# Two-layer trunk: the handovers between mixer and MLP issued in another order

## The chip, the cores and the metric

The kernel runs on one NeuronCore of a Trainium2 chip. Its metric is the time of one execution on the device, in microseconds (us). Three executions before the change took 1163.44, 1163.95 and 1166.36 us; the median is 1163.95.

## The reference, cut to what matters

512 tokens of 1024 features pass two residual layers. Layer 0 mixes the tokens by latent attention with 16 heads, layer 1 by an mLSTM with 4 heads; after each mixer stands an MLP.

```python
for i in range(DEPTH):                       # 0: attention, 1: mLSTM
    x = x + mixer_i(rms_norm(x, norm_mix[i]))        # ends in  ... @ w_o
    x = x + square(relu(rms_norm(x, norm_ffn[i]) @ w1[i])) @ w2[i]   # 1024 -> 4096 -> 1024
```

`rms_norm(x, g)` is `x * rsqrt(mean(x*x) + 1e-6) * g`. The mLSTM's head output is normalised the same way, per head, and multiplied by a sigmoid gate before `w_o`.

## The kernel before, in words

**Numbers and tiles.** Everything is fp32. A product is made of three matmuls in a rounded format: each operand is split into a high part (a copy, on ScalarE) and a low part (what is left, a subtraction on VectorE), and the three products high by high, high by low, low by high are summed (`mm3`). So each weight tile of 128x1024 goes through a load (SyncE queue, tag `wr`, 3 buffers), a copy to `wh` and a subtraction to `wl` (3 buffers each), and each activation through the same two steps.

**The residual stream** lies in `xs[t, f]`: four blocks of 128 tokens by two halves of 512 features. A matmul needs the features on the partitions, so at each handover TensorE turns `xs` by transposes against the identity (`turn`). `Norm.half(th, m)` turns the features of m and m+1 for the two token blocks of half `th` into one PSUM bank (4 transposes), and then, for each of the two features' 256 columns, copies them out on ScalarE with the gain (`hi`) and subtracts on VectorE (`lo`). `Norm.square(t, f)` sums the squares of one `xs` tile on ScalarE; `stat` and a reciprocal or power make the factor of the norm from the sums, which is applied after the product, to its rows.

**Handover from mixer to MLP** (`out_proj`, then the head of `ffn`). `out_proj` multiplies by `w_o` in two halves f of the output; `z0`, `z1` are the four PSUM banks of each half (`mm` has 3 banks, `tp` 4, `po` 1). In layer 0 most of half 0 (`zo`) was done beside the attention. A last loop over the four token blocks t finishes both halves, adds them to `xs`, takes the squares, starts the first `w1` tile after t = 0 and turns the first two blocks after t = 2. `norm.tail` holds the turns of the last two blocks; `ffn` does these around the first products: `w1` tiles 0 and 1 by token halves (`HALVES`), then whole tiles in the loop over `units`: F units (one `w1` tile: 24 matmuls of 512 columns) and P units (one of the seven products of a block scheme on `w2`, 24 matmuls of 512 columns). In that loop `ahead` loads and splits weights two to four units early, `f_post` takes relu and square, GpSimd sums the parts that the scheme needs, and `y_add` adds a product to `xs` with the factor `r2`.

**Handover from MLP to mLSTM.** The last `w2` block runs as four plain products (`l_mm`), n = 0 to 3, of two token blocks each; the first turns for the mLSTM (`half(0, ...)`, `half(1, (0, 2))`) stand between them, the rest in `mlstm` after the first value product. In layer 1 the same places turn the result for the output (`out`).

**The mLSTM's heads** end in a normalisation: the numerators' sums go through a chain of small instructions on VectorE and GpSimd, `hb` is scaled, and 8 transposes turn it (line 1146) for the output projection.

**What sets the order.** Instructions issued through `ipe`, `idve`, `iact`, `ipool` (while on) stay behind the instruction that the program issued before them on the same engine. All others are placed by a planner in the framework, by simulated times; it also assigns the buffers. The framework makes two instructions on the same PSUM bank wait for each other when they run on different engines. `ipe` and `idve` are always on, `iact` in the last loop of `out_proj`, in `ffn` and around the tail in `mlstm`. The loads stand on the SyncE queue in the planner's order.

Of the kernel before, what the change touches and what calls it, by code (L numbers as in the profile page):

```python
# [61 lines left out]
def trunk(ctx: ExitStack, tc, a, yT, dbg=None):  # L62
# [173 lines left out]
    class Norm:  # L236
# [13 lines left out]
        def half(self, th, m, bank=ps_mm):  # L250

            ps, c = bank(), HALVES[th]
            for n in range(2):
                for t in range(2):
                    turn(ps, (2 * n + t) * P, m + n, 2 * th + t)
            for n in range(2):
                g, p_ = cst[:, self.gcol + m + n:self.gcol + m + n + 1], ps[:, n * 256:(n + 1) * 256]
                hi, lo = self.hi[m + n], self.lo[m + n]
                iact.activation(hi[:, c], p_, AF.Copy, scale=g)
                idve.scalar_tensor_tensor(lo[:, c], p_, g, hi.bitcast(F32)[:, c], op0=mult, op1=sub)  # L260
# [28 lines left out]
    def mla(mp):  # L289
# [378 lines left out]
        out_proj(a["w_oa"], oT, 0, zo, wo[3])  # L668
# [6 lines left out]
    def out_proj(wsrc, lhs, layer, z0=None, w0=None):  # L675
# [7 lines left out]
        for j in range(3):  # L683
            for f, z in todo:
                w = load_w(wsrc[f, j], D)
                for t in range(NB):
                    for k in (2 * j, 2 * j + 1):
                        o_mm(z[t], w, k, t, lhs, ipe)
        last = [(z0, w0, (KD - 1,)) if w0 else (z0, load_w(wsrc[0, 3], D), (KD - 2, KD - 1)),
                (z1, load_w(wsrc[1, 3], D), (KD - 2, KD - 1))]  # L690
        norm = Norm(C_NF + layer * KD)
        iact.on = True
        for t in range(NB):
            for z, w, ks in last:
                for k in ks:
                    o_mm(z[t], w, k, t, lhs, ipe)
            for f, (z, _, _) in enumerate(last):
                idve.tensor_add(xs[t, f], xs[t, f], z[t])
            if t == 0:
                norm.first = split_w(load_raw(a["w1"][layer, 0], D), D, iact, idve)  # L700
            elif t == 2:
                for m in range(0, KD, 2):
                    norm.half(0, m)
            for f in range(2):
                norm.square(t, f)
        norm.tail = [lambda m=m: norm.half(1, m, ps_tp) for m in range(0, KD, 2)]
        iact.on = False
        norms.append(norm)

# [3 lines left out]
    def ffn(fp, layer, last):  # L713
# [166 lines left out]
        ws["F", 0] = norm.first  # L880
        f_load(1)
# [3 lines left out]
        for do in norm.tail[:2]:  # L885
            do()
        f_split(1)
        f_mm(ps[1], 1, HALVES[0])
        for do in norm.tail[2:]:
            do()  # L890
        u_ = norm.stat()
        idve.reciprocal(r2, u_)
# [12 lines left out]
        for s_ in range(2, len(units)):  # L905
# [11 lines left out]
            if u[0] == "F":  # L917
                f_post(ps, u[1])
            else:
# [26 lines left out]
        for n, (th, f) in enumerate(((0, 0), (0, 1), (1, 0), (1, 1))):  # L946
            bank["L", f] = [ps_tp(), ps_tp()]
            for t in range(2):
# [23 lines left out]
    def mlstm(lp):  # L972
# [62 lines left out]
        for h in range(MH):  # L1035
# [7 lines left out]
            for t in range(NB):  # L1043
# [97 lines left out]
            nc.vector.tensor_scalar_mul(gh, cst[:, C_HN + 2 * h:C_HN + 2 * h + 2], 0.5)  # L1141
            for n in range(2):
# [10 lines left out]
        out_proj(a["w_ob"], [(out_h[m // 4][:, m % 4], out_l[m // 4][:, m % 4]) for m in range(KD)], 1)  # L1153
# [100 lines left out]
```

## Time and profile before

| | before |
|---|---|
| median of three executions | 1163.95 us |
| the profiled execution's own time | 1163.95 us |
| its span, first to last instruction | 1161.9 us |
| TensorE matmuls busy | 1121.3 us, 97% |
| VectorE busy | 826.9 us, 71% |
| ScalarE busy | 556.4 us, 48% |
| GpSimd busy | 455.7 us, 39% |
| mean granted TensorE clock | 0.994 of full speed |

Busy time is the union of an engine's instructions; what is left of the span is the time in which the engine stood. Matmuls overlap, so the distance between the starts of two like groups tells more than the duration of one. The rows on which the prediction rests stand two sections below.

### The profile page before, as it was taken

Reading aid. Unit: us, or ns where it says so; the run is one execution under the profiler, and the core shown is the slowest. Engines: PE = TensorE matmul, PEld = TensorE weight load, DVE = VectorE, ACT = ScalarE, POOL = GpSimd, SP = SyncE. Lnnn points to the kernel's source line nnn. Section 1 sums busy time; section 2 is a strip of 40 time slices with the busy share of each in tenths; the row PEclk is TensorE's granted clock in tenths of the full one; section 3 lists DMA queues with packets and bytes.
Section 4 is the critical chain, followed back from the end, with each engine's and each line's share of the span. In section 5 each row is a group of like instructions: output and inputs, shape, how many; then the busy total and the mean of one; then the engine's idle time right before and its main releaser. Section 6 shows DMA issues by size and latency. Waiting matters only on the chain.

```text
span 1161.9 us, 15626 instructions
## 1 busy us (share of the span) xinstructions
PE 1121.3 (97%) x5802; PEld 954.0 (82%) x5802; DVE 826.9 (71%) x1284; ACT 556.4 (48%) x969; POOL 455.7 (39%) x453
## 2 busy tenths in 40 slices
PE   7899999989999999999999999989899999999998
PEld 7889987878888888888788898877788888888886
DVE  7689997356798789778666565534478788779863
ACT  4578776345544435444454343323454444444451
POOL 6677775107356337434001011100255347436500
PEclk9999999999999999999999999999999999999999
DMA  5301111423432343343113222322532433343212
GB/s 200 111 24 47 37 56 46 137 73 128 127 104 79 108 124 89 96 111 108 37 56 90 73 73 73 91 59 69 162 92 74 127 109 91 91 127 94 70 55 73
DMA packets 32427, 104.27 MB, mean 90 GB/s; under 512 B 3424, under 2 KB 6752, under 8 KB 32352
## 3 DMA queue, kind: packets, MB, share of 16 engines
q1 hardware_dynamic: 32352, 103.27, 29.3%
q8 instruction: 46, 0.75, 0.3%
q14 instruction: 29, 0.24, 0.1%
HBM read 101.16 MB, written 2.10 MB: 89 GB/s over the span
## 4 chain that ended last, share of the span: by engine, by line
PE 89%; DVE 4%; ACT 2%; POOL 2%; issue 1%; DMA 1%; SPq 0%; ACTq 0%; POOLq 0%; DVEq 0%
PE mm L80 38%; PE tp L80 36%; PE mm L174 4%; PE mm L176 4%; PE mm L175 3%; PE po L80 3%; DVE xg L80 1%; DVE wl L80 1%; ACT xg L80 1%; DVE x L80 1%; PE tp L176 1%; PE tp L175 1%; PE tp L174 1%; ACT t L80 1%; POOL x L80 0%
## 5 line engine op out<-in xcount | busy, mean ns | idle before, releaser
L80 PE MATMUL mm<-xg,wh 128*128 128x512 f32 (+1 forms) x1088 | 322.9, 380 | 7.4 <-ACT wh L80 7.1
L80 POOL TENSOR_TENSOR z<-z 128x256 f32<-128x256 f32 x112 | 131.4, 1193 | 344.7 <-ACT z L80 342.5
L80 PEld LDWEIGHTS mm<-xg,wh 128*128 128x128 f32 x1088 | 202.7, 191 | 46.0 <-ACT wh L80 7.6
L80 DVE TENSOR_TENSOR wl<-tw,wh 128x1024 fp32r<-128x1024 f32 x102 | 173.1, 1697 | 74.2 <-ACT wh L80 74.2
L80 PE MATMUL mm<-xg,wl 128*128 128x512 f32 (+1 forms) x544 | 207.9, 382 | 1.5 <-DVE wl L80 1.5
L80 POOL TENSOR_TENSOR tw<-tw,tw 128x1024 f32<-128x1024 f32 x56 | 158.9, 2846 | 30.4 <-issue 29.2
L80 PE MATMUL tp<-wh,hl 128*128 128x512 f32 x424 | 165.2, 390 | 0.5 <-DVE hl L80 0.5
L80 PE MATMUL tp<-wh,hh 128*128 128x512 f32 x424 | 165.4, 390 | 0.0
L80 PE MATMUL tp<-wl,hh 128*128 128x512 f32 x424 | 165.0, 389 | 0.0
L80 DVE TENSOR_TENSOR wl<-wr,wh 128x1024 fp32r<-128x1024 f32 (+1 forms) x72 | 121.3, 1685 | 49.9 <-ACT wh L80 49.9
L80 DVE SCALAR_TENSOR_TENSOR x<-tp,r,x 128x512 f32<-128x512 f32 (+1 forms) x215 | 149.5, 733 | 9.0 <-PE tp L80 8.8
L80 ACT ACTIVATE t<-mm 128x512 f32<-128x512 f32 (+3 forms) x97 | 54.3, 560 | 200.9 <-PE mm L80 191.8
L80 ACT CAST wh<-tw 128x1024 fp32r<-128x1024 f32 x102 | 106.8, 1047 | 36.7 <-PE tp L80 28.9
L80 PEld LDWEIGHTS mm<-xg,wl 128*128 128x128 f32 x544 | 103.7, 191 | 24.8 <-DVE wl L80 6.5
L164 DVE TENSOR_TENSOR wl<-wr,wh 128x1024 fp32r<-128x1024 f32 (+2 forms) x44 | 52.7, 1199 | 60.8 <-ACT wh L160 60.7
L80 PEld LDWEIGHTS tp<-wh,hl 128*128 128x128 f32 x424 | 79.6, 188 | 18.0 <-DVE hl L80 1.4
L80 ACT CAST wh<-wr 128x1024 fp32r<-128x1024 f32 (+1 forms) x74 | 78.8, 1065 | 32.1 <-PE tp L80 27.7
L80 PEld LDWEIGHTS tp<-wh,hh 128*128 128x128 f32 x424 | 79.6, 188 | 17.1 <-issue 0.8
L80 PEld LDWEIGHTS tp<-wl,hh 128*128 128x128 f32 x424 | 79.6, 188 | 16.4
L80 DVE TENSOR_TENSOR hl<-z,hh 128x1024 fp32r<-128x1024 f32 (+1 forms) x60 | 85.2, 1420 | 3.4 <-ACT hh L80 3.4
L160 ACT CAST wh<-wr 128x1024 fp32r<-128x1024 f32 (+2 forms) x44 | 43.9, 997 | 87.3 <-PE po L80 31.3
L80 ACT CAST hh<-z 128x1024 fp32r<-128x1024 f32 (+1 forms) x60 | 56.9, 949 | 57.2 <-POOL z L80 57.2
(271 smaller groups left out, 2041.9 us busy)
## 6 DMA issues: line engine op xcount, KB each, us to landing
wr<-in_w SPq DMA_DIRECT2D x64, 512.0 KB, 3.6
tw<-in_w SPq DMA_DIRECT2D x64, 512.0 KB, 3.6
wr<-in_w_qkv SPq DMA_DIRECT2D x8, 640.0 KB, 4.0
wr<-in_w_oa SPq DMA_DIRECT2D x8, 512.0 KB, 3.7
wr<-in_w_mo SPq DMA_DIRECT2D x8, 512.0 KB, 3.6
wr<-in_w_ob SPq DMA_DIRECT2D x8, 512.0 KB, 3.6
wr<-in_w_v SPq DMA_DIRECT2D x6, 512.0 KB, 4.0
wr<-in_w_z SPq DMA_DIRECT2D x8, 336.0 KB, 4.8
```

What stands on the lines that cost most here:

```text
L80: return lambda *args, **kw: tc.keep_in_program_order(f(*args, **kw)) if self.on else f(*args, **kw)
L160: act.copy(hi[:, :n], raw[:, :n])
L164: dve.tensor_sub(lo[:, :n], raw[:, :n], hi[:, :n].bitcast(F32))
L174: pe.matmul(out, lhsT=lh, rhs=rh, start=start, stop=False)
L175: pe.matmul(out, lhsT=lh, rhs=rl, start=False, stop=False)
L176: pe.matmul(out, lhsT=ll, rhs=rh, start=False, stop=stop)
```

## The change

No computation is added or left out; instructions stand elsewhere.

1. `Norm.half`: both ScalarE copies of a bank come before both VectorE subtractions (before: copy, subtraction, copy, subtraction).
2. `out_proj` becomes a generator that yields after each weight tile; its loops run over f outside and j inside. Without a given `w0` (layer 1) that tile is split into a buffer of another tag (`big`).
3. Last loop of `out_proj`: two `w1` tiles are split there (after t = 0 and t = 1), not one; only block 0 is squared; the turns of m = 6 move from after t = 2 to between the two halves of t = 3.
4. Head of `ffn`: all four tail turns after the first half unit; the split of the second tile is gone from here. The squares of blocks 1 to 3 follow the posts of F units 2 to 4, the reciprocal `r2` the last of them.
5. End of `ffn`: `y_add` comes before the turns; the four turns of half 0 are shared between t = 0 and t = 1 of n = 2; the squares move to n = 3 and, for the last two, into `mlstm` behind the tail. The `w2` tile `b21` is split into the tag `z`, not `wh`/`wl`.
6. `mlstm`, last head: `out_proj` is started before the last transposes, with its first weight tile (24 matmuls); these transposes are kept in program order behind it.

```diff
@@ Norm.half
-            for n in range(2):
-                g, p_ = ...
-                hi, lo = self.hi[m + n], self.lo[m + n]
+            parts = [(self.hi[m + n], self.lo[m + n], cst[...], ps[:, n * 256:(n + 1) * 256]) for n in range(2)]
+            for hi, lo, g, p_ in parts:
                 iact.activation(hi[:, c], p_, AF.Copy, scale=g)
+            for hi, lo, g, p_ in parts:
                 idve.scalar_tensor_tensor(lo[:, c], p_, g, hi.bitcast(F32)[:, c], op0=mult, op1=sub)
@@ out_proj
-        for j in range(3):
-            for f, z in todo:
+        for f, z in todo:
+            for j in range(3):
                 w = load_w(wsrc[f, j], D)
                 for t in range(NB):
                     for k in (2 * j, 2 * j + 1):
                         o_mm(z[t], w, k, t, lhs, ipe)
-        last = [(z0, w0, (KD - 1,)) if w0 else (z0, load_w(wsrc[0, 3], D), (KD - 2, KD - 1)),
-                (z1, load_w(wsrc[1, 3], D), (KD - 2, KD - 1))]
+                yield
+        if not w0:
+            w0 = split_w(load_raw(wsrc[0, 3], D), D, to=big(F32R).rearrange("p (c j) e -> c p (j e)", c=2))
+            ks = (KD - 2, KD - 1)
+        else:
+            ks = (KD - 1,)
+        last = [(z0, w0, ks), (z1, load_w(wsrc[1, 3], D), (KD - 2, KD - 1))]
...
         for t in range(NB):
-            for z, w, ks in last:
+            for f, (z, w, ks) in enumerate(last):
                 for k in ks:
                     o_mm(z[t], w, k, t, lhs, ipe)
+                if t == 3 and f == 0:
+                    norm.half(0, 6)
             for f, (z, _, _) in enumerate(last):
                 idve.tensor_add(xs[t, f], xs[t, f], z[t])
-            if t == 0:
-                norm.first = split_w(load_raw(a["w1"][layer, 0], D), D, iact, idve)
+            if t < 2:
+                norm.first.append(split_w(load_raw(a["w1"][layer, 2 * t], D), D, iact, idve))
+                for f in range(2 - 2 * t):
+                    norm.square(t, f)
             elif t == 2:
-                for m in range(0, KD, 2):
+                for m in (0, 2, 4):
                     norm.half(0, m)
-            for f in range(2):
-                norm.square(t, f)
@@ ffn, head
-        ws["F", 0] = norm.first
-        f_load(1)
+        ws["F", 0], ws["F", 1] = norm.first
         f_load(2)
         ps = [ps_mm(), ps_mm()]
         f_mm(ps[0], 0, HALVES[0])
-        for do in norm.tail[:2]:
+        for do in norm.tail:
             do()
-        f_split(1)
         f_mm(ps[1], 1, HALVES[0])
-        for do in norm.tail[2:]:
-            do()
-        u_ = norm.stat()
-        idve.reciprocal(r2, u_)
@@ ffn, loop over units
                 f_post(ps, u[1])
+                if s_ < 5:
+                    norm.square(s_ - 1, 0)
+                    norm.square(s_ - 1, 1)
+                    if s_ == 4:
+                        idve.reciprocal(r2, norm.stat())
...
-                        l_split("b21", False)
+                        l_split("b21", True)
@@ ffn, end
-                if n == 2 and t == 0:
-                    half(0, (0, 2, 4, 6))
+                y_add(2 * th + t, f, bank["L", f][t])
+                if n == 2:
+                    half(0, ((0, 2), (4, 6))[t])
                 if n == 3 and t == 0:
                     half(1, (0, 2))
-                y_add(2 * th + t, f, bank["L", f][t])
-                if not last:
-                    nxt.square(2 * th + t, f)
+                if not last and n < 2:
+                    nxt.square(t, f)
+                if not last and n == 3:
+                    nxt.square(2 + t, 0)
@@ mlstm, after the first value product
                     for do in norm.tail:
                         do()
+                    for i in range(2):
+                        norm.square(2 + i, 1)
@@ mlstm, end of a head
+            if h == MH - 1:
+                proj_b = out_proj(a["w_ob"], [(out_h..., out_l...) for m in range(KD)], 1)
+                next(proj_b)
             for n in range(2):
...
-                    pe.transpose(ps[:, i * P:(i + 1) * P], hb[i // 2][:, o:o + P], ident)
+                    (ipe if h == MH - 1 else pe).transpose(ps[:, i * P:(i + 1) * P], hb[i // 2][:, o:o + P], ident)
...
-        out_proj(a["w_ob"], [(out_h..., out_l...) for m in range(KD)], 1)
+        for _ in proj_b:
+            pass
```

## Rows read from the trace of the kernel before

**Rows 1.** The page: busy time of each engine, share of span, instructions.

```profile
PE 1121.3 (97%) x5802; PEld 954.0 (82%) x5802; DVE 826.9 (71%) x1284; ACT 556.4 (48%) x969; POOL 455.7 (39%) x453
```

**Rows 2.** Windows: stretch, its us, busy of PE PEld DVE ACT POOL, PEclk, DMA.

```profile
239.94:265.50 25.56, 19.69 (x138) 18.23 (x137) 12.38 (x25) 13.51 (x29) 0.00 (x0) 0.93 0.26 78
254.00:256.00 2.00, 1.90 (x9) 1.90 (x10) 0.05 (x1) 0.00 (x0) 0.00 (x0) 0.50 0.51 80
258.17:258.96 0.79, 0.79 (x11) 0.79 (x9) 0.00 (x0) 0.16 (x1) 0.00 (x0) 1.00 0.00 0
262.64:265.50 2.86, 2.86 (x26) 2.86 (x25) 1.60 (x2) 2.19 (x4) 0.00 (x0) 1.00 0.25 36
285.00:577.89 292.89, 292.89 (x1285) 240.44 (x1284) 233.03 (x210) 137.25 (x167) 128.03 (x75) 1.00 0.33 98
577.89:593.01 15.12, 11.45 (x61) 9.27 (x60) 8.58 (x15) 8.47 (x18) 0.91 (x2) 1.00 0.22 69
593.01:757.22 164.21, 164.20 (x983) 145.59 (x981) 95.17 (x240) 67.06 (x132) 18.36 (x29) 1.00 0.25 75
757.22:769.07 11.85, 8.28 (x33) 6.75 (x34) 4.93 (x16) 2.08 (x5) 1.01 (x1) 0.86 0.11 39
805.15:831.43 26.28, 20.68 (x141) 18.95 (x140) 12.50 (x25) 13.62 (x29) 0.00 (x0) 0.94 0.23 63
```

**Rows 3.** Timeline, TensorE, first MLP handover: start, us, [idle before <- releaser].

```profile
242.74 0.63 PE L80 MATMUL mm<-cst,x 128*128 128x128 f32 x4 [1.33 <-DVE xg L80]
...
252.84 0.51 PE L80 MATMUL mm<-xg,wh 128*128 128x256 f32 x2 [3.64 <-ACT wh L80]
254.10 0.58 PE L80 MATMUL mm<-xg,wl 128*128 128x256 f32 x1 [0.75 <-DVE wl L80]
```

**Rows 4.** Waits of TensorE, second MLP handover, 805 to 832 us.

```profile
PE mm L80 <- ACT wh L80: 3.5, 1, 3.5
```

**Rows 5.** Timeline, all engines, the copies of the turned banks.

```profile
241.60 0.84 ACT L80 ACTIVATE xg<-mm,cst 128x256 fp32r<-128x256 f32 x2 [0.55 <-DVE xg L80]
242.11 0.88 DVE L80 SCALAR_TENSOR_TENSOR xg<-mm,cst,xg 128x256 fp32r<-128x256 f32 x2 [0.54 <-ACT xg L80]
...
243.02 0.47 ACT L80 ACTIVATE xg<-mm,cst 128x256 fp32r<-128x256 f32 x1 [0.58 <-DVE xg L80]
```

**Rows 6.** Timeline, SyncE queue, ahead of the second MLP handover.

```profile
788.16 13.79 SPq L150 DMA_DIRECT2D wr<-in_w  x3
```

**Rows 7.** Timeline, all engines, handover from MLP to mLSTM.

```profile
580.69 0.30 PE L80 MATMUL mm<-cst,x 128*128 128x128 f32 x1 [1.33 <-DVE xg L80]
...
585.43 1.22 DVE L164 TENSOR_TENSOR wl<-wr,wh 128x1024 fp32r<-128x1024 f32 x1
...
587.98 1.40 DVE L80 SCALAR_TENSOR_TENSOR x<-tp,r,x 128x512 f32<-128x512 f32 x2
...
588.87 0.30 PE L80 MATMUL mm<-cst,x 128*128 128x128 f32 x1 [2.08 <-DVE x L80]
```

**Rows 8.** Timeline, all engines, the last head's transposes.

```profile
760.79 1.14 PE L1146 MATMUL tp<-cst,hb 128*128 128x128 f32 x8 [3.59 <-DVE hb L1139]
```

**Rows 9.** Chain that ended last, start of the mLSTM's output projection.

```profile
761.93 5.74 PE mm L80 x18
767.67 1.40 PE po L80 x6
```

**Rows 10.** Groups, ScalarE: the squares, all 24; busy, mean ns.

```profile
L80 ACT ACTIVATE t<-x 128x512 f32<-128x512 f32 x24 | 15.1, 628 | 21.6 <-DVE x L80 21.6
```

**Rows 11.** Timeline, all engines, ahead of the first P unit.

```profile
277.38 3.38 POOL L80 TENSOR_TENSOR tw<-tw,tw 128x1024 f32<-128x1024 f32 x1
...
278.86 2.98 DVE L80 TENSOR_TENSOR wl<-wr,wh 128x1024 fp32r<-128x1024 f32 x1 [0.36 <-ACT wh L80]
...
283.31 0.50 PE L80 MATMUL tp<-wh,hl 128*128 128x512 f32 x1 [0.16 <-DVE hl L80]
```

**Rows 12.** Waits of TensorE, end of the kernel, 1144 to 1162 us.

```profile
PE mm L80 <- DVE x L80: 1.5, 3, 0.9
```

More of the change, by code (lines that the diff above doesn't have):

```diff
@@ L255, in half @@
                     turn(ps, (2 * n + t) * P, m + n, 2 * th + t)
-            for n in range(2):
-                g, p_ = cst[:, self.gcol + m + n:self.gcol + m + n + 1], ps[:, n * 256:(n + 1) * 256]
-                hi, lo = self.hi[m + n], self.lo[m + n]
+            parts = [(self.hi[m + n], self.lo[m + n], cst[:, self.gcol + m + n:self.gcol + m + n + 1],
+                      ps[:, n * 256:(n + 1) * 256]) for n in range(2)]
+            for hi, lo, g, p_ in parts:
                 iact.activation(hi[:, c], p_, AF.Copy, scale=g)
+            for hi, lo, g, p_ in parts:
                 idve.scalar_tensor_tensor(lo[:, c], p_, g, hi.bitcast(F32)[:, c], op0=mult, op1=sub)
@@ L667, in mla @@
         load_x()
-        out_proj(a["w_oa"], oT, 0, zo, wo[3])
+        for _ in out_proj(a["w_oa"], oT, 0, zo, wo[3]):
+            pass
     def o_mm(ps, w, k, t, lhs, pe=nc.tensor):
@@ L688, in out_proj @@
                         o_mm(z[t], w, k, t, lhs, ipe)
-        last = [(z0, w0, (KD - 1,)) if w0 else (z0, load_w(wsrc[0, 3], D), (KD - 2, KD - 1)),
-                (z1, load_w(wsrc[1, 3], D), (KD - 2, KD - 1))]
+                yield
[5 more added lines that the diff above has]
+        last = [(z0, w0, ks), (z1, load_w(wsrc[1, 3], D), (KD - 2, KD - 1))]
         norm = Norm(C_NF + layer * KD)
+        norm.first = []
         iact.on = True
         for t in range(NB):
-            for z, w, ks in last:
+            for f, (z, w, ks) in enumerate(last):
                 for k in ks:
                     o_mm(z[t], w, k, t, lhs, ipe)
+                if t == 3 and f == 0:
+                    norm.half(0, 6)
             for f, (z, _, _) in enumerate(last):
                 idve.tensor_add(xs[t, f], xs[t, f], z[t])
-            if t == 0:
-                norm.first = split_w(load_raw(a["w1"][layer, 0], D), D, iact, idve)
+            if t < 2:
+                norm.first.append(split_w(load_raw(a["w1"][layer, 2 * t], D), D, iact, idve))
+                for f in range(2 - 2 * t):
+                    norm.square(t, f)
             elif t == 2:
-                for m in range(0, KD, 2):
+                for m in (0, 2, 4):
                     norm.half(0, m)
-            for f in range(2):
-                norm.square(t, f)
         norm.tail = [lambda m=m: norm.half(1, m, ps_tp) for m in range(0, KD, 2)]
@@ L708, in out_proj @@
         norms.append(norm)
+        yield
     norms = []
@@ L1141, in mlstm @@
             nc.vector.tensor_scalar_mul(gh, cst[:, C_HN + 2 * h:C_HN + 2 * h + 2], 0.5)
+            if h == MH - 1:
+                proj_b = out_proj(a["w_ob"], [(out_h[m // 4][:, m % 4], out_l[m // 4][:, m % 4]) for m in range(KD)], 1)
+                next(proj_b)
             for n in range(2):
@@ L1152, in mlstm @@
                 nc.vector.scalar_tensor_tensor(ol, t_, gh[:, n:n + 1], oh.bitcast(F32), op0=mult, op1=sub)
-        out_proj(a["w_ob"], [(out_h[m // 4][:, m % 4], out_l[m // 4][:, m % 4]) for m in range(KD)], 1)
+        for _ in proj_b:
+            pass
     with stage("mlap") as pool:
```

## The prediction

> **What bounds the kernel now.** I read four views. The page first: TensorE is busy for 1121.3 of the 1161.9 us of the span, the next engine for 826.9 [rows 1]. So only the 40.6 us in which TensorE stands, and what a lowered clock adds, can be won by moving work. The windows second, one for each stage, to see where it stands: in the first MLP's loop (285.00 to 577.89) and in the mLSTM (593.01 to 757.22) it never does; four short stretches hold it, the two handovers from mixer to MLP (25.56 and 26.28 us long), the one from MLP to mLSTM (15.12) and the end of the last head (11.85) [rows 2]. Third, TensorE's timeline and waits within these: what ended each gap [rows 3, 4, 7, 8]. Last, ScalarE and VectorE in the same moments, for what those had in front of them [rows 5, 7, 11]. The change touches just these four stretches, the squares and the kernel's end.
>
> **Prices.** Eight turns take 0.79 us, so one 0.1; a half unit of 24 matmuls of 256 columns takes 2.86 [rows 2]; six matmuls of 512 columns take 1.40, so one 0.233 [rows 9]. TensorE's clock: in 254 to 256 us, behind the gap of 3.64 us, the granted clock is 0.50, the 1.2 GHz level, where the stretches without a gap have 1.00 [rows 2, 3]; behind the last head's gap 18 matmuls take 5.74 us where three times 1.40 would be 4.20, so such a gap costs some 1.5 us more than itself [rows 9].
>
> **Part 1, copies grouped.** Today ScalarE's copy waits 0.55 us for VectorE's subtraction of the same bank, and that 0.54 us for the copy; from one pair of copies to the next, a bank, pass 1.42 us (241.60 to 243.02) [rows 5]. Grouped, a bank costs ScalarE 0.84 and VectorE 0.88, on different banks at once: 0.9 a bank, four banks in 4.4 us in place of some 6.3. By itself that moves nothing; it decides what the next parts wait for.
>
> **Parts 3 and 4, handover to the first MLP (239.94 to 265.50).** TensorE's work in it: 32 turns (3.2), the products of t = 3 (9 matmuls, 2.1), four half units (11.4): 16.7 us of 25.56. It loses 1.33 at the turns of m = 6, which want a fourth `mm` bank, and 3.64 + 0.75 at the second half unit, whose weight's copy and subtraction stand behind the tail's copies [rows 3]; the rest is the low clock behind that. After the change I lay it out from 239.94: 12 turns to 241.2; the three products of half 0 at t = 3 to 241.9; the bank of m = 0, turned at 240.4, comes free at 242.4 (its copies 0.84, its subtractions 0.88, some 0.3 of handing over), so a wait of 0.5 stays; turns and six products to 244.3; half unit to 247.2; 16 turns to 248.8; the second half unit to 251.6, its weight split by 240.1, since the `wh` buffer comes free when the last loop begins; the tail's eight half copies are done by 252.0, the second-half products take feature after feature from 251.6, so nothing waits; two half units more: the first whole unit starts at 257.4, not 265.5. **Gain 8.1.** Bounds: 4.4 if only the wait for the weight goes, 8.9 if no wait stays.
>
> **The same for the second MLP (805.15 to 831.43).** The wait for the weight is 3.5 [rows 4]. Twelve products at t = 3 (2.8), 3.2 and 11.4 make 17.4; six products stand before the turns of m = 6, so their bank is free in time; 0.3 of small waits: 17.7 of 26.28. **Gain 8.6**, bounds 3.5 and 8.9. Its loads: by 801.6 all of the first four `w1` tiles were issued (the second at 788.16, three issues in 13.79 us) [rows 6], ahead of the handover, so the earlier split finds its data, and the next loads come no later, since they wait for subtractions that come earlier. Nothing on GpSimd's queue moves: its sums begin behind the post of F unit 1, which stays.
>
> **Part 5, handover to the mLSTM (577.89 to 593.01).** Three groups of 12 products (8.4) and 24 turns (2.4) are 10.8 of 15.12 us. Lost: 1.33 for the fourth bank, and 2.08 and more at 588.87, where the turns of half 1 wait for `y_add`, which stood behind two weight subtractions (1.22 each) and three of the turns' own on VectorE [rows 7]. With two banks, 2.8 us of products, then two banks, no bank is awaited; with `y_add` ahead of the copies (0.7 each [rows 7]) the sums that half 1 turns are done some 2.7 us before it. The mLSTM's own weights may still put one subtraction of 1.22 there; that slack covers it. **Gain 4.3**, bounds 1.3 and 4.6. The squares moved behind the tail feed factors for blocks 2 and 3, which are used two value products (some 6 us) later than block 0's; two squares are 1.3 us: no cost. `b21` in another buffer lets the first value weights be split early: no cost, no term.
>
> **Part 6, last head.** TensorE waits 3.59 us for `hb` [rows 8]. 24 matmuls are 5.6 us, longer than the wait. At 761.93 they start without a wait for their weight [rows 9]; that it is there 4.7 us earlier I take, since it is the stage's first; the lower bound is for the case that it isn't. 5.6 + 0.8 stand for the 11.85 us from 757.22 to 769.07 [rows 2], where turns and the same 24 matmuls ran, half of them at the low clock. **Gain 5.4**, bounds 0 (the matmuls don't run there) and 5.4. The other order of f and j costs nothing: one weight per 5.6 us either way.
>
> **End of the kernel.** Three waits for `y_add`, 1.5 in all [rows 12]; the last, before the final turns, stays; two go, and the turns stand better. **Gain 1.0**, bounds 0 (the output copies still wait for buffers) and 1.5.
>
> **What the squares cost.** In each MLP six squares of 0.63 us [rows 10] move to F units 2 to 4, behind the post, ahead of the next copy on ScalarE's in-order queue. Two take 1.3 us with their reads. Behind unit 3 this has no cover: today ScalarE's copy of the next weight comes straight after the post, VectorE's subtraction runs 278.86 to 281.84, the second one follows, and the first P unit already waits 0.16 for it at 283.31 [rows 11]. Moved by 1.3 it waits 1.3 longer. **Cost 1.3 in each MLP, 2.6.** Bounds: 0, if the subtraction meets less of GpSimd's work and shortens from 2.98 toward the 1.22 that the same form takes at 585.43 [rows 7, 11]; 3.1, if it meets as much again (1.3 + 1.76). I take 1.3, the value between, since GpSimd's instruction of 3.38 lies before the subtraction as well as beside it [rows 11].
>
> The Trainium skill's page "SBUF — State Buffer", "Who interferes with whom", says that a VectorE instruction with two SBUF inputs and a GpSimd instruction that reads SBUF exclude each other, the later one waiting for the whole of the earlier. The row of 2.98 beside GpSimd's 3.38 agrees with waiting. By that rule a shift of 1.3 us can fall on either side of one GpSimd instruction, so it speaks for the upper bound as much as for 0; that case is the second rival.
>
> **The sum.** 8.1 + 8.6 + 4.3 + 5.4 + 1.0 - 2.6 = 24.8. The profiled execution's own time is 1163.95, the median of the runs: 1163.95 - 24.8 = 1139.1, forecast **1139**.
>
> **Rivals.**
> 1. *The re-plan uncovers the mLSTM* (slower than before). Its 983 matmuls and most VectorE instructions are placed by the planner, and all start some 11 us earlier in its simulation, with other buffers free. For: the last head shows what a bare chain costs, 3.59 + 1.5 = 5.1 us. Against: the stretch has no idle time now [rows 2], its order follows program priorities, and its first products are the same. Place: the chains between projections, scores, numerators and transposes. Each that is uncovered costs 5.1; from five on the change loses (5 x 5.1 = 25.5). With eight, two in each head: 1180.
> 2. *The first P unit waits longer*: 3.1 in each MLP in place of 1.3 gives 1142.7; if the lateness also reaches the second P unit (GpSimd's sums to ScalarE to VectorE), up to 1145.
> 3. *The low clock stays.* The new handovers put 16 turns in a row, and their waits of 0.2 to 0.5 us are not the only ones. If the clock falls to 1.2 GHz there as behind the old gaps, 1.5 us in each of four places: 1145. Against: it was 1.00 over the 24 turns and the 2.08 us gap of the mLSTM handover [rows 2, 7].
> 4. *The last head's matmuls don't cover it* (their bank or weight is late, so that the change doesn't do what it says there): 5.4 lost, 1144.5. Against: they are held behind the last numerator only, and `mm` and `po` are then free.
>
> **How the numbers follow.** Forecast with its own range 1135 to 1142: 0.57. Rival 2: 0.14; rival 3: 0.09; rival 4: 0.06; of rival 1 one to three chains (1144 to 1154) 0.05, four or five (1160 to 1165) 0.02, more 0.03. The rest, 0.04, has the squares at no cost and the upper bounds of the gains (1133 to 1135). The range of eight in ten, 1133 to 1148, takes in the forecast and rivals 2 to 4, with room for a part that each mis-sizes, and leaves out most of rival 1. About 0.3%, 3.5 us, is what can be told from no change. Faster by more than that 0.95 (all but rival 1's far parts), the same 0.02 (four or five chains), slower 0.03.
>
> **What would show it.** Right: the two MLP handovers are 17 to 18 us from the end of t = 2 to the first whole unit, with no wait for `wh`; the second half unit runs at clock 1.00; a bank's copies come 0.9 apart; behind the last numerator come projection matmuls, and no wait on line 1146; the mLSTM handover is about 10.8. The squares: a wait of some 1.5 us for `hl` at the first P unit of each MLP. Wrong: a wait for `xg` or `x` longer than 1 us in a handover, idle time in the mLSTM, a P unit waiting 3 us, or a stretch of clock 0.5 behind 805 us.

## The result, and the profile after

The changed kernel takes 1137.05 us (median of four executions, 1136.99 to 1137.65), the kernel before beside it 1164.96 (four, 1163.44 to 1166.36): a ratio of 0.9762, interval 0.9745 to 0.9779. The forecast was 1139, its range 1133 to 1148. The profiled execution took 1137.65 us with a span of 1135.8; the spans differ by 26.1 us, the own times by 26.3, where the sum said 24.8. That execution is the slowest of its four, 0.6 us above their median.

The page after, busy time of each engine ([rows 1] before):

```profile
PE 1113.4 (98%) x5802; PEld 949.7 (84%) x5802; DVE 824.1 (73%) x1284; ACT 553.0 (49%) x969; POOL 455.1 (40%) x453
```

The instruction counts are the same. TensorE stands for 22.4 us of the span, where it stood for 40.6.

Windows of the kernel after, in the columns of [rows 2]:

```profile
240.01:257.63 17.62, 17.32 (x138) 16.54 (x137) 10.65 (x23) 9.26 (x20) 0.00 (x0) 1.00 0.41 138
257.63:273.98 16.35, 16.35 (x74) 13.53 (x73) 9.86 (x6) 11.38 (x20) 13.48 (x8) 1.00 0.44 161
273.98:570.43 296.45, 296.02 (x1297) 242.63 (x1296) 237.60 (x216) 141.53 (x175) 131.24 (x78) 1.00 0.33 100
570.43:581.27 10.84, 10.84 (x62) 9.29 (x60) 8.28 (x16) 6.98 (x17) 0.91 (x2) 1.00 0.17 48
581.31:745.50 164.19, 164.19 (x984) 145.78 (x983) 94.00 (x238) 66.69 (x133) 18.45 (x29) 1.00 0.26 75
745.50:751.90 6.40, 6.40 (x33) 5.31 (x32) 2.60 (x12) 1.56 (x4) 1.01 (x1) 1.00 0.15 61
787.96:805.86 17.90, 17.90 (x142) 17.19 (x140) 9.95 (x21) 9.26 (x20) 0.00 (x0) 1.00 0.37 118
```

The first, fourth, sixth and last of these are the four stretches that held TensorE's idle time. They are 17.62, 10.84, 6.40 and 17.90 us, where they were 25.56, 15.12, 11.85 and 26.28. In three of them busy time equals length, and the granted clock is 1.00 in all (it was 0.93, 1.00, 0.86 and 0.94). The mLSTM is as long as before, 164.19 for 164.21.

TensorE's timeline in the first MLP handover of the kernel after. It answers to [rows 3]:

```profile
242.54 0.63 PE L80 MATMUL mm<-cst,x 128*128 128x128 f32 x4 [0.30 <-DVE xg L80]
...
247.26 1.91 PE L80 MATMUL tp<-cst,x 128*128 128x128 f32 x16
```

The 1.33 us for a bank have become 0.30, and the waits for the second weight, 3.64 and 0.75, are gone: behind the 16 turns nothing is awaited. ScalarE and VectorE in the same moments, the rows that answer to [rows 5]:

```profile
240.65 2.29 ACT L80 ACTIVATE xg<-mm,cst 128x256 fp32r<-128x256 f32 x6 [2.19 <-PE mm L80]
...
241.52 2.44 DVE L80 SCALAR_TENSOR_TENSOR xg<-mm,cst,xg 128x256 fp32r<-128x256 f32 x6
```

Three banks go through without a stop: 2.29 / 3 = 0.76 us a bank on ScalarE, 0.81 on VectorE, where a pair of copies came every 1.42 us.

The last head, TensorE ([rows 8] before), and the first and last turns of the output, after and then before:

```profile
745.28 0.39 PE L80 MATMUL mm<-wh,big 128*128 128x512 f32 x1
...
750.87 1.03 PE L80 MATMUL tp<-cst,hb 128*128 128x128 f32 x8
...
1118.99 1.03 PE L80 MATMUL mm<-cst,x 128*128 128x128 f32 x8
...
1131.39 0.63 PE L80 MATMUL mm<-cst,x 128*128 128x128 f32 x4 [0.93 <-DVE x L80]
```

```profile
1144.05 1.93 PE L80 MATMUL mm<-cst,x 128*128 128x128 f32 x16
...
1157.50 0.63 PE L80 MATMUL mm<-cst,x 128*128 128x128 f32 x4 [0.94 <-DVE x L80]
```

The projection's 24 matmuls start straight behind the last numerator, the turns follow them without a wait. At the end only the wait before the last turns is left; 13.45 us from the first turns to the last are now 12.40.

What got worse is small: from the first whole F unit to the mLSTM handover, second and third window, 312.80 us (before 312.39, from [rows 2]: 265.50 to 577.89), and 313.13 in the second MLP, 805.86 to 1118.99 (before 312.62, 831.43 to 1144.05). All engines ahead of the first P unit after, against [rows 11]:

```profile
266.76 2.99 DVE L80 TENSOR_TENSOR wl<-tw,wh 128x1024 fp32r<-128x1024 f32 x1 [3.53 <-ACT wh L80]
...
269.83 3.32 POOL L80 TENSOR_TENSOR tw<-tw,tw 128x1024 f32<-128x1024 f32 x1 [1.16 <-DVE wl L80]
...
272.26 1.97 DVE L80 TENSOR_TENSOR wl<-wr,wh 128x1024 fp32r<-128x1024 f32 x1 [1.38 <-ACT wh L80]
...
275.71 0.50 PE L80 MATMUL tp<-wh,hl 128*128 128x512 f32 x1 [0.43 <-DVE hl L80]
```

The P unit waits 0.43 us where it waited 0.16, and 0.87 in the second MLP (0.36 before). Not all of the 0.87 is the squares'. In this execution GpSimd stood 1.31 us in the second MLP for a load (before: 1.13); in the profile of the changed kernel run again (last line) it did not, and the wait is 0.47:

```profile
815.77 6.05 POOL L80 TENSOR_TENSOR tw<-tw,tw 128x1024 f32<-128x1024 f32 x2 [1.31 <-DMA tw<-in_w]
...
820.49 2.41 DVE L80 TENSOR_TENSOR wl<-wr,wh 128x1024 fp32r<-128x1024 f32 x1 [0.94 <-ACT wh L80]
...
824.37 0.50 PE L80 MATMUL tp<-wh,hl 128*128 128x512 f32 x1 [0.87 <-DVE hl L80]
```

```profile
823.37 0.50 PE L80 MATMUL tp<-wh,hl 128*128 128x512 f32 x1 [0.47 <-DVE hl L80]
```

By the two profiles the squares cost 0.3 us in the first MLP and 0.1 to 0.5 in the second, not 1.3 each; the runs on the squares below narrow the second to about 0.3.

| term of the sum | predicted | measured in the traces |
|---|---|---|
| handover to the first MLP | 8.1 | 25.56 - 17.62 = 7.9 |
| handover to the second MLP | 8.6 | 26.28 - 17.90 = 8.4 |
| handover to the mLSTM | 4.3 | 15.12 - 10.84 = 4.3 |
| last head | 5.4 | 11.85 - 6.40 = 5.4 |
| end of the kernel | 1.0 | 13.45 - 12.40 = 1.0 |
| squares | -2.6 | -0.4 - 0.5 = -0.9 |
| sum | 24.8 | 26.1 |

The row of the squares is what both MLPs have lost in length, and its second number holds the late load too. In the other profile of the changed kernel the same stretches are 312.75 and 312.84 us long, 0.4 and 0.2 more than before.

### The profile page after: what moved, and what is told of

Read it like the earlier page. It is cut to its first block, busy times and chain, and to the rows that moved or that the text cites. A ratio compares the mean times of both kernels' runs of the same rounds, so it can differ in the third digit from the quotient of the medians.

```text
span 1135.8 us, 15650 instructions
## 1 busy us (share of the span) xinstructions
PE 1113.4 (98%) x5802; PEld 949.7 (84%) x5802; DVE 824.1 (73%) x1284; ACT 553.0 (49%) x969; POOL 455.1 (40%) x453
## 4 chain that ended last, share of the span: by engine, by line
PE 93%; DVE 3%; POOL 2%; ACT 1%; issue 1%; DMA 0%; SPq 0%; ACTq 0%; POOLq 0%; DVEq 0%
PE mm L80 39%; PE tp L80 38%; PE mm L174 4%; PE mm L176 4%; PE mm L175 4%; PE po L80 3%; PE tp L176 1%; PE tp L175 1%; PE tp L174 1%; DVE wl L80 1%; ACT t L80 1%; DVE x L80 1%; POOL x L80 0%; POOL scr L80 0%; DMA x<-in_xT 0%
## 5 line engine op out<-in xcount | busy, mean ns | idle before, releaser
L80 PE MATMUL mm<-xg,wh 128*128 128x512 f32 (+1 forms) x1088 | 319.2, 377 | 0.0
L80 PEld LDWEIGHTS mm<-xg,wh 128*128 128x128 f32 x1088 | 200.2, 188 | 37.3
L80 PE MATMUL tp<-wh,hl 128*128 128x512 f32 x408 | 159.0, 390 | 1.3 <-DVE hl L80 1.3
L80 PE MATMUL tp<-wh,hh 128*128 128x512 f32 x408 | 159.1, 390 | 0.0
L80 PE MATMUL tp<-wl,hh 128*128 128x512 f32 x408 | 158.8, 389 | 0.0
L80 PEld LDWEIGHTS tp<-wh,hl 128*128 128x128 f32 x408 | 76.6, 188 | 18.0 <-DVE hl L80 2.1
L80 PEld LDWEIGHTS tp<-wh,hh 128*128 128x128 f32 x408 | 76.6, 188 | 16.5 <-ACT zw L80 0.8
L80 PEld LDWEIGHTS tp<-wl,hh 128*128 128x128 f32 x408 | 76.6, 188 | 15.8
L80 DVE TENSOR_TENSOR hl<-z,hh 128x1024 fp32r<-128x1024 f32 (+1 forms) x60 | 82.9, 1382 | 0.0
```

Source lines behind the costliest of these rows:

```text
L80: return lambda *args, **kw: tc.keep_in_program_order(f(*args, **kw)) if self.on else f(*args, **kw)
```

## Experiments: the parts one by one

All times are medians of four executions, all edits are to the changed kernel unless said otherwise. The kernel before, run seven times beside each set, took 1166.54, 1163.6, 1165.98 and 1165.77 us in the four sets; the changed kernel again took 1136.93. The four differ by 2.9 us, so a difference of a microsecond between kernels of different sets is read from the traces, not from the medians. One stretch that no edit touches differs too: from 60 to 80 us the granted clock is 0.91 in the profile of the changed kernel and 1.00 in some of the others.

**Grouping undone.** Copy, subtraction, copy, subtraction again:

```diff
-            for hi, lo, g, p_ in parts:
                 idve.scalar_tensor_tensor(lo[:, c], p_, g, ...)
```

> The changed kernel with one part undone: in each turned bank copy, subtraction, copy, subtraction again. Theory A (each part gives its own term; the grouping itself is worth little and only decides small waits): a bank takes 1.42 us again, the additions of token block 3 end some 0.8 us after TensorE wants to turn it, the fourth bank comes 0.3 us later, so 1.1 to 1.3 us in each of the two MLP handovers and nothing at the mLSTM: about 1139.5 us. Theory B (the other parts rest on the grouping, their gains go without it): waits of 3 us and more in each handover, and the low clock behind them: 1147 us or more.

Measured: 1137.73 (1137.37 to 1138.81), ratio 0.9757 (0.9742 to 0.9771). Its turns of m = 6 and its first handover, timeline and window:

```profile
242.91 0.63 PE L80 MATMUL mm<-cst,x 128*128 128x128 f32 x4 [0.75 <-DVE xg L80]
```

```profile
239.93:258.08 18.15, 17.40 (x138) 16.54 (x137) 11.32 (x23) 10.03 (x20) 0.00 (x0) 1.00 0.34 110
```

The first handover is 0.53 us longer, the second (17.91) and the mLSTM's (10.83) are not. In the changed order the grouping is worth half a microsecond: theory A in kind (the wait for the fourth bank, in place of waits of 3 us), but less than half of what it expected in the first handover and nothing in the second.

**Last head undone.** The projection starts behind the turns again:

```diff
-                next(proj_b)
...
-                    (ipe if h == MH - 1 else pe).transpose(...)
+                    pe.transpose(...)
```

> The changed kernel with one part undone: the output projection starts behind the last head's transposes, which the planner places. Theory A (the 24 matmuls cover a wait of 3.6 us, and the clock stays up, 1.5 us): 5.4 us are lost again, 1142.5 us, with the granted clock at 0.5 some 2 us behind the gap. Rival B (the low clock behind the gap is not the gap's doing): 3.6 us, 1140.7 us, and full clock behind the gap. Rival C (the cover was worth nothing, its matmuls only changed places): 1137 us.

Measured: 1143.15 (1140.53 to 1143.71), ratio 0.9803 (0.9787 to 0.982): 6.1 us above the changed kernel. The wait is back. Timeline and a window behind it, in the one execution that was profiled:

```profile
748.31 1.14 PE L1162 MATMUL tp<-cst,hb 128*128 128x128 f32 x8 [3.59 <-DVE hb L1153]
```

```profile
750.00:752.00 2.00, 2.00 (x10) 1.65 (x9) 1.80 (x4) 1.34 (x2) 0.00 (x0) 1.00 0.00 0
```

That execution took 1140.53, 2.9 above the changed kernel's profiled one: the clock stayed at 1.00 behind the gap. It is 2.9 and not 3.6 because it came to the last head 0.7 us sooner (its clock is 1.00 from 60 to 80 us as well, and a wait at the kernel's start is 0.4 us shorter). The other three took 1142.87 to 1143.71. So the wait is worth some 3.6 us, and 2.3 to 3.2 more come in some executions. Their mean granted clock is 0.995 and 0.996, that of the profiled one 1.000, so a lower clock is in them; how much of it stands behind the gap, no trace of this kernel shows. The profiled execution is rival B's (1140.7, full clock), the median theory A's (1142.5); rival C is out.

**Second `w1` split late.** The split of the second tile, with its load, goes back between the tail's turns, two before and two after it:

```diff
-            if t < 2:
-                norm.first.append(split_w(load_raw(a["w1"][layer, 2 * t], D), ...))
+            if t == 0:
+                norm.first.append(split_w(load_raw(a["w1"][layer, 0], D), ...))
...
-        for do in norm.tail:
+        for do in norm.tail[:2]:
             do()
+        f_split(1)
         f_mm(ps[1], 1, HALVES[0])
+        for do in norm.tail[2:]:
+            do()
```

> The changed kernel with one part undone: the second MLP weight is split again inside the MLP's head, between two and two of the tail's turns. Theory A (in the MLP handovers the gain is that weight's wait): TensorE waits 2.4 us for its copy and some 1 us for its subtraction, then 0.8 us for the last tail bank; 4.1 us in each MLP, 1145.3 us, and 1148.5 us if the clock falls to 1.2 GHz behind the wait. Theory B (with grouped copies and without squares in ScalarE's queue the weight would have come in time anyway): under 1 us in each, 1139 us.

Measured: 1146.25 (1145.84 to 1146.77), ratio 0.9828 (0.9814 to 0.9843). TensorE's waits in the first handover, and a window behind them:

```profile
PE mm L80 <- ACT wh L80: 2.2, 1, 2.2
PE mm L80 <- DVE wl L80: 0.8, 1, 0.8
```

```profile
251.00:255.00 4.00, 4.00 (x22) 4.00 (x22) 0.00 (x0) 0.00 (x0) 0.00 (x0) 0.57 0.44 131
```

22.57 us for 17.62, and 22.83 for 17.90: 4.9 us in each handover, of which 3.0 are the waits. Most of the rest is the clock behind them: 4.00 us at 0.57 do the work of 2.3, which is 1.7 lost in the first handover (an estimate from that window). Theory A, between its two numbers: without this part 9.9 of the 16.3 us that both handovers gain are lost.

**Additions after the turns**, at the end of the MLP, as before:

```diff
-                y_add(2 * th + t, f, bank["L", f][t])
-                if n == 2:
-                    half(0, ((0, 2), (4, 6))[t])
+                if n == 2 and t == 0:
+                    half(0, (0, 2, 4, 6))
                 if n == 3 and t == 0:
                     half(1, (0, 2))
+                y_add(2 * th + t, f, bank["L", f][t])
```

> The changed kernel with one part undone: at the end of each MLP the four turns of half 0 stand together again and the additions behind them. Theory A (the parts are independent, each as sized): the handover to the mLSTM takes 4.2 us longer and the end of the kernel 0.8 us, 1142 us. Theory B (most of this gain was the grouping's, since grouped copies free the fourth bank and let the additions come sooner): 0.3 to 2 us at the handover, 1138 to 1139.5 us in all.

Measured: 1139.98 (1139.49 to 1140.34), ratio 0.9774 (0.976 to 0.9789). Its handover to the mLSTM, timeline:

```profile
573.35 0.63 PE L80 MATMUL mm<-cst,x 128*128 128x128 f32 x4 [1.06 <-DVE xg L80]
```

The handover is 12.08 us, 1.24 longer; the wait for the sums, 2.08 in [rows 7], doesn't come back with the old order. At the end two short waits return (0.55 and 0.27), and the first to last turns of the output take 13.67 us, 1.3 more. Theory B for the handover (0.3 to 2); the end lost 0.5 more than expected. So the old order costs 1.2 us in this handover when the copies are grouped, and leaving the copies apart costs nothing there when the order is new (10.83): each remedy does most of the work alone.

**Grouping alone**, on the kernel before:

```diff
-            for n in range(2):
-                g, p_ = ...; hi, lo = ...
+            parts = [(hi, lo, g, p_) for n in range(2)]
+            for hi, lo, g, p_ in parts:
                 iact.activation(hi[:, c], p_, AF.Copy, scale=g)
+            for hi, lo, g, p_ in parts:
                 idve.scalar_tensor_tensor(lo[:, c], p_, g, ...)
```

> The kernel before with the grouping of the copies alone. Theory A (the remedies overlap: alone the grouping frees the fourth bank sooner in both MLP handovers and in the mLSTM handover, and lets the second weight's split come sooner because it stands behind fewer microseconds of copies): the mLSTM handover 15.1 to about 12.1 as in the run with late sums, each MLP handover 2 to 4 us shorter: 7.0 to 11.0 in all, 1153 to 1157 where the kernel before is 1164. Theory B (grouping by itself moves nothing, as the prediction says, and as its removal from the changed kernel, which cost 0.5 us, suggests): 1163 or more.

Measured: 1154.97 (1154.65 to 1156.22), ratio 0.9919 (0.9903 to 0.9935), 8.6 us below the kernel before. Windows of its three handovers:

```profile
239.35:262.60 23.25, 19.28 (x139) 18.23 (x138) 11.88 (x25) 12.87 (x29) 0.00 (x0) 0.93 0.29 91
575.12:587.22 12.10, 11.04 (x61) 9.32 (x60) 9.13 (x17) 8.18 (x18) 0.91 (x2) 1.00 0.29 79
...
800.38:822.84 22.46, 18.62 (x142) 17.30 (x141) 11.96 (x25) 12.97 (x29) 0.00 (x0) 1.00 0.29 83
```

2.3, 3.0 and 3.8 us are gone. In both MLP handovers the second weight's copy is still waited for, 2.15 us in place of 3.6 and 3.5, and the fourth bank 1.06 and 0.93 in place of 1.3 and 1.2; at the mLSTM handover the wait for the sums is gone. Not all of the 3.8 is the waits': behind the same 2.15 us the clock fell in the first handover (0.93 over it) and stayed at 1.00 in the second, where the kernel before had 0.94. That is some 1.6 us (an estimate, 0.06 of 26.28). Theory A is right, and the prediction's "by itself that moves nothing" is wrong: the same edit is worth 8.6 us in the old order and 0.5 in the new one.

## Experiments: the squares

**Squares of 8 columns** where they stand, behind F units 2 to 4:

```diff
-            iact.activation(j, xs[t, f], AF.Square, ...)
+            iact.activation(j[:, :n], xs[t, f][:, :n], AF.Square, ...)
...
-                    norm.square(s_ - 1, 0)
+                    norm.square(s_ - 1, 0, 8)
```

> The changed kernel with the squares behind F units 2 to 4 reduced to 8 of 512 columns; the rest of those sums of squares is left out, so this run prices the squares where they now stand. Theory A (the trace after: the first P unit waits 0.43 us and 0.87 us where it waited 0.16 and 0.35, so the squares cost 0.3 and 0.5): both waits fall back to about 0.16 and 0.35, gain 0.3 to 0.8, about 1136.5. Theory B (the 1.3 us a MLP of the prediction, paid partly in places that the P unit's wait does not show): the stretch from the last F unit to the second P unit shortens by more than a microsecond in each MLP, about 1134.5. Theory C (the wait is made by the splits of weights alone): no change, 1137.

Measured: 1136.31 (1136.04 to 1136.68), ratio 0.9756 (0.9738 to 0.9774). Ahead of its first P unit, VectorE, GpSimd and TensorE:

```profile
263.69 9.09 POOL L80 TENSOR_TENSOR tw<-tw,tw 128x1024 f32<-128x1024 f32 x3
...
271.31 2.55 DVE L80 TENSOR_TENSOR wl<-wr,wh 128x1024 fp32r<-128x1024 f32 x1 [0.80 <-ACT wh L80]
...
275.33 0.50 PE L80 MATMUL tp<-wh,hl 128*128 128x512 f32 x1 [0.15 <-DVE hl L80]
```

The waits are 0.15 and 0.20; theory A. Against the changed kernel's two profiles (0.43 and 0.87, 0.43 and 0.47) the squares cost 0.3 us in the first MLP and, without the late load, 0.3 in the second. GpSimd's three sums run without the 1.16 us that it waited for VectorE after the change.

**Only the squares behind unit 3 short**, the ones directly ahead of the subtraction:

```diff
-                    norm.square(s_ - 1, 0)
+                    norm.square(s_ - 1, 0, 8 if s_ == 3 else T)
```

> The changed kernel with the two squares behind F unit 3 alone reduced to 8 of 512 columns; the rest of their sums is left out, and the squares behind units 2 and 4 are whole. In every trace so far VectorE's weight subtraction in front of the first P unit ends 1.08 us after GpSimd's running sum, whenever it began. Theory A (the wait of the first P unit is set by the end of GpSimd's sum, and that is late because the squares behind unit 2 delay the subtraction that GpSimd waits for): the subtraction begins 0.8 to 1.0 us earlier and takes that much longer, still ends 1.08 us after GpSimd's sum, and the wait of 0.43 us in the first MLP stays: 1137. Theory B (the squares behind unit 3 delay the subtraction directly, as the prediction counted): it ends earlier, and the waits fall to 0.16 and 0.35 us or below: 1136.3.

Measured: 1137.08 (1136.27 to 1137.86), ratio 0.9757 (0.9741 to 0.9773). The same place:

```profile
269.36 3.32 POOL L80 TENSOR_TENSOR tw<-tw,tw 128x1024 f32<-128x1024 f32 x1 [1.16 <-DVE wl L80]
...
270.95 2.81 DVE L80 TENSOR_TENSOR wl<-wr,wh 128x1024 fp32r<-128x1024 f32 x1 [0.54 <-ACT wh L80]
...
275.24 0.50 PE L80 MATMUL tp<-wh,hl 128*128 128x512 f32 x1 [0.43 <-DVE hl L80]
```

After the change the subtraction began 1.72 us ahead of the P unit (273.98 - 272.26) and took 1.97; here it begins 2.56 ahead (273.51 - 270.95) and takes 2.81. It ends at the same distance, and the wait of 0.43 stays; in the second MLP it is 0.48, as in the changed kernel run again (0.47). Theory A: these two squares cost nothing.

**All squares back in the last loop** of each output projection, six more in each than the changed kernel has there, and none behind F units:

```diff
                 norm.first.append(...)
-                for f in range(2 - 2 * t):
-                    norm.square(t, f)
             elif t == 2:
                 for m in (0, 2, 4):
                     norm.half(0, m)
+            for f in range(2):
+                norm.square(t, f)
...
+        idve.reciprocal(r2, norm.stat())
```

> The changed kernel with all eight squares back in the last loop of each output projection and the reciprocal in the head of the MLP. Theory A (ScalarE has room between the grouped copies: six squares of 0.63 us, 3.8 us in all, delay the copies of the turned banks by part of that): handover 0.5 to 1.5 us longer in each MLP, the waits of the first P unit 0.3 and 0.5 us shorter, net 0 to 2 us slower, 1137 to 1139. Theory B (the squares stand in front of the fourth bank's copies as the weight's split did, and the whole 3.8 us ends on TensorE, with a low clock behind it): 2.5 us or more in each MLP, 1142 or more.

Measured: 1136.12 (1135.83 to 1136.27), ratio 0.9755 (0.974 to 0.977), below both expectations. ScalarE in its first handover, and the two handovers' windows:

```profile
240.11 2.30 ACT L80 ACTIVATE xg<-mm,cst 128x256 fp32r<-128x256 f32 x6 [0.78 <-PE mm L80]
242.26 0.67 ACT L80 ACTIVATE t<-x 128x512 f32<-128x512 f32 x1
...
245.95 0.63 ACT L80 ACTIVATE t<-x 128x512 f32<-128x512 f32 x1 [1.60 <-DVE x L80]
```

```profile
239.47:257.09 17.62, 17.32 (x139) 16.54 (x137) 11.19 (x26) 11.71 (x28) 0.00 (x0) 1.00 0.42 137
787.08:804.97 17.89, 17.89 (x141) 17.18 (x140) 10.46 (x24) 11.71 (x28) 0.00 (x0) 1.00 0.38 119
```

The squares fall between the copies of one block and the next, and both handovers are as long as without them. Moving the squares away was not needed. It cost 0.9 us by the medians, which are of two sets; by the waits of the first P units, 0.16 and 0.20 here, it cost 0.5 against the changed kernel run again.

**The same with the copies apart**, as in the first experiment:

> Squares in the last loop of each output projection, and the copies of a turned bank one half at a time as in the kernel before; all else as changed. Theory A (it is the grouping, 0.9 us a bank in place of 1.4, that makes room on ScalarE for the squares): the handovers grow by 1 to 3 us each where the grouping's removal alone cost 0.53 and 0.12 us, 1138.5 to 1142. Theory B (the squares lie where ScalarE idles in either case, behind the additions of each block): about 0.6 above the squares in the loop with grouped copies, 1136.7.

Measured: 1141.02 (1140.95 to 1141.61), ratio 0.9787 (0.977 to 0.9803), 4.1 above the changed kernel run again in the same set, and 4.9 above the squares in the loop with grouped copies, which ran in another. ScalarE and the windows:

```profile
241.68 0.84 ACT L80 ACTIVATE xg<-mm,cst 128x256 fp32r<-128x256 f32 x2 [0.73 <-DVE xg L80]
243.10 0.84 ACT L80 ACTIVATE xg<-mm,cst 128x256 fp32r<-128x256 f32 x2 [0.58 <-DVE xg L80]
...
244.89 0.62 ACT L80 ACTIVATE t<-x 128x512 f32<-128x512 f32 x1
...
247.19 0.47 ACT L80 ACTIVATE xg<-mm,cst 128x256 fp32r<-128x256 f32 x1 [0.61 <-DVE xg L80]
```

```profile
239.84:259.75 19.91, 18.77 (x138) 16.83 (x137) 11.80 (x26) 12.48 (x28) 0.00 (x0) 1.00 0.32 99
789.80:809.47 19.67, 19.34 (x141) 17.40 (x140) 11.16 (x24) 12.48 (x28) 0.00 (x0) 1.00 0.29 87
```

The copies are back at 1.42 us a bank, the squares come in among the later ones, and the handovers are 2.3 and 1.8 us longer. Theory A. So grouping and moving the squares are two remedies for one thing, ScalarE's time between the last products and the next: with either, the other is worth little (grouping 0.5 us, moving the squares less than nothing), without both 4.1 us are lost in the handovers.

## Experiments: a version that beats both

**Parts first.** Behind F unit 4 the split of the P unit's operand (`hl`) comes ahead of the weight's two units on:

```diff
-            ahead(s_)
+            if s_ != 4:
+                ahead(s_)
             s_now[0] = s_
             while later and later[0][0] <= s_:
                 later.pop(0)[1]()
+            if s_ == 4:
+                ahead(s_)
```

> The changed kernel with one order turned in each MLP: behind F unit 4 the split of the first P weight comes ahead of the split for the unit after it. Theory A (the first P unit waits for its own weight's subtraction, which stands behind the other weight's and behind the squares): the waits of 0.43 and 0.87 us go, the next unit's weight is still in time, 1.0 to 1.3 us gained, about 1136. Theory B (the other weight, now last, makes the unit after it wait as long): no change, 1137, with the wait one unit later.

The expectation names the wrong thing: what the P unit waits for, and what the edit moves ahead, is not its weight but its operand `hl`. That this stands behind the other weight's subtraction is as it says. Measured: 1135.65 (1134.89 to 1135.93), ratio 0.975 (0.9735 to 0.9765). VectorE ahead of its first P unit:

```profile
271.58 1.92 DVE L80 TENSOR_TENSOR hl<-z,hh 128x768 fp32r<-128x768 f32 x1 [1.16 <-ACT hh L80]
273.42 1.76 DVE L80 TENSOR_TENSOR wl<-wr,wh 128x1024 fp32r<-128x1024 f32 x1
```

`hl` is done by 273.50, the P unit (273.51) waits for nothing, and in the list of TensorE's waits `hl` has gone (1.3 us after the change). Theory A.

**Both**, squares in the loop and parts first, and **the changed kernel again** beside it:

> Two variants at once: all squares in the last loop of each output projection, and behind F unit 4 the first P weight's split ahead of the next one. Theory A (both remove the same wait of the first P unit, 0.43 and 0.87 us; the squares in the loop leave 0.16 and 0.20 of it, the order all): no more than 0.4 us below the better of the two alone, 1135.3 to 1136. Theory B (they remove different waits and add up): 1134.2 or less.

> The changed kernel itself, unedited, beside the two variants on the same chip. Theory A: 1137, with the variant of both edits 1.2 to 1.8 us below it. Theory B (the differences of about a microsecond seen so far were between chips or calls): both within 0.4 us.

Measured: 1135.31 (1135.0 to 1136.36), ratio 0.9738 (0.9724 to 0.9753), and 1136.93 (1136.56 to 1137.4), ratio 0.9751 (0.9736 to 0.9765). Theory A: the two edits remove the same wait, and the wait for `hl` is gone. Both together are 1.6 us below the changed kernel of the same set. This is the lowest median, but parts first alone (1134.89 to 1135.93, in another set) cannot be told from it.

## Why the prediction was right, and where it was not

**The four stretches: right, by their steps.** The work that was laid out for TensorE filled them: 17.4 and 17.7 us said, 17.62 and 17.90 measured; 10.8 said, 10.84 measured; 6.4 and 6.40. The wait for the bank of m = 0, put at 0.5, is 0.30. That the first weight tile of the last projection would be there 4.7 us earlier, which was taken without a row, holds. One bound was wrong: 4.6 for the mLSTM handover is more than the 4.3 that its own layout leaves (15.12 - 10.8).

**Part 1, "by itself that moves nothing": wrong.** The prediction gave the fourth bank's and the second weight's waits to the parts that reorder the turns and the split. The grouped kernel before shows that shorter copies alone bring back 8.6 us in the same handovers, some 1.6 of them by a clock that stayed up in one: what stands behind the copies is less late when these are short (the second weight's copy 2.15 us in place of 3.6 and 3.5), and the sums at the mLSTM handover come in time. The sum was right for the whole change only because the gain was counted once, from the layout of each stretch, and not as a sum over edits.

**The squares: the mis-sized term.** "Moved by 1.3 it waits 1.3 longer" failed; some 0.3 in each MLP stand in its place (0.4 and 0.5 by the table, a late load included), so by the table 1.7 us more were gained than the sum had, against 0.4 less in the two MLP handovers. The subtraction did begin 1.27 us later as said (1.72 us ahead of the P unit, where it was 281.85 - 278.86 = 2.99), but it took 1.01 less. In [rows 11] its 2.98 us end 1.08 after GpSimd's 3.38 (277.38 + 3.38 = 280.76; 278.86 + 2.98 = 281.84), so from its beginning to 280.76 it was waiting, and a later begin came out of that wait. The prediction had this case as its lower bound, the subtraction that shortens, and gave it up for the value between. What the P unit pays in the first MLP is GpSimd's own lateness: the squares behind unit 2 push the subtraction at 266.76 behind a sum of GpSimd's, and GpSimd then waits 1.16 us for its end. With unit 3's squares short the wait stays, with all short it goes, and unit 4's begin at 275.41, after the subtraction: unit 2's are left.

The Trainium skill's page "SBUF — State Buffer", "Who interferes with whom", says that of the two engines the one that issues second is fully blocked, not slowed. The traces agree: what is left of the subtraction after the sum is 1.08 us each time. The prediction read this rule as speaking for the upper bound as much as for nothing; placed on the row, it says from where the subtraction runs, and gives the cost of unit 3's squares as 0, as measured (0.43 us with them and without).

**The low clock.** The 1.5 us put behind the last head's gap is an amount of that profiled execution, not of the gap: behind the same 3.59 us the run with the last head undone kept 1.00.

**The rivals.** The mLSTM was not uncovered (164.19 us, all of it busy). The first P unit never came to 3.1. The granted clock is 1.00 in every window of the kernel after, so no low clock stayed in what the change touches. The last head's matmuls cover its chain in full.

## What to carry to other kernels

Price a change by laying out each stretch anew, not by adding what each edit is worth: the same grouping was worth 8.6 us in one order (some 1.6 of them the clock) and 0.5 in another. When an instruction is long because another engine holds it, look for what it ends behind; moving its beginning within that wait was free here. Before moving small work out of a busy place, see whether another edit of the same change makes room for it there.

## What the runs showed of the hardware

**A VectorE subtraction beside a GpSimd sum ends 1.08 us after it, wherever in the sum it began.** The 128x1024 subtraction ahead of the first P unit, in six places:

| kernel | begins | takes | ends | GpSimd's sum ends | difference |
|---|---|---|---|---|---|
| before, first MLP | 278.86 | 2.98 | 281.84 | 280.76 | 1.08 |
| after, first MLP | 272.26 | 1.97 | 274.23 | 273.15 | 1.08 |
| after, second MLP | 820.49 | 2.41 | 822.90 | 821.82 | 1.08 |
| squares of 8 columns | 271.31 | 2.55 | 273.86 | 272.78 | 1.08 |
| unit 3's squares short | 270.95 | 2.81 | 273.76 | 272.68 | 1.08 |
| squares in the loop | 270.43 | 2.99 | 273.42 | 272.34 | 1.08 |

Alone the same form takes 1.22 us [rows 7]. So it makes next to no headway while the sum runs (0.14 of its 1.22), and its length says nothing of its own price. GpSimd waits in the same way: its sum takes 2.40 us alone, and 3.32 after the change, where VectorE's `hl` subtraction runs from 269.67 to 270.88 across its beginning at 269.83.

**The same gap lowers the clock in one execution and not in another.** The last head's wait is 3.59 us in three traces: the kernel before [rows 8], the run with the last head undone, and the grouped kernel before. Behind it the second of these has the clock at 1.00 in its window above. The kernel before has 0.57, and the grouped kernel before, below its wait, 0.58:

```profile
762.00:764.00 2.00, 2.00 (x7) 1.58 (x6) 1.81 (x3) 1.33 (x2) 0.00 (x0) 0.57 0.00 0
```

```profile
754.99 1.94 PE L1147 MATMUL tp<-cst,hb 128*128 128x128 f32 x8 [3.59 <-DVE hb L1140]
```

```profile
754.00:762.00 8.00, 7.01 (x23) 5.94 (x24) 3.84 (x8) 1.33 (x2) 0.46 (x1) 0.58 0.00 0
```

Two waits of 2.2 and 0.8 us close together were enough for 0.57 in the run with the second weight late; the same two in the second handover of the grouped kernel before left it at 1.00, as 2.08 did at the old mLSTM handover [rows 2, 7]. What decides is not shown. One profiled execution doesn't tell what such a gap costs on average.
